# Constant products at the start, keys split out of PSUM, a sink column, and norm work on POOL, in a one-core decoder layer

## The chip, the core and the metric

The kernel runs on one core of a Trainium2 chip. The metric is the device time of one execution in microseconds. Five engines work beside one another, each with its own queue, in order: TensorE (PE in the profile; its weight loads are PEld), VectorE (DVE), ScalarE (ACT), GpSimd (POOL) and SyncE (SP), which here only issues transfers. Everything is f32; the large products use fp32r, a form that TensorE takes in one pass, and each operand is split into a high and a low part so that three products (high x high, high x low, low x high) keep the precision. Plain f32 products take two passes, which the profile counts as two instructions.

## The reference

One decoder layer on a sequence of 2048 positions with 1024 features: a conditioned RMSNorm, one projection into eleven groups of columns, a gated linear attention (4 heads), a sliding-window attention (8 query heads, 2 key heads, window 128) with a sink logit per head, an output projection with a gate, a residual and a last RMSNorm. What the change touches:

```python
mod = silu(c) @ w_ada + b_ada;  shift, scale, gate = split(mod, 3)
h = rmsnorm(x, g_norm) * (1 + scale) + shift
proj = h @ w_in                       # gq gk gv ga gz sq sk sv sz
...
q, k = rope(sq), rope(sk)
scores = where(valid, q @ k.T * hd ** -0.5, -inf)      # blocks of 128 queries, 256 keys
probs = softmax(concat([scores, sink], -1), -1)[..., :-1]
o_swa = (probs @ v) * silu(sz)
...
x = x + gate * (concat([o_gla, o_swa]) @ w_out);  out = rmsnorm(x, g_final)
```

## The kernel before

The sequence is cut into four units of 512 positions (u = 0 to 3), each of four tiles of 128 (t). A unit runs its projections slot by slot, in `ORDER0` for the first unit and `ORDER` for the others; when the slots that an attention needs are there, its tiles follow. In the end `out_tile` runs the output projection for 16 tiles (products py).

**The order of the work.** No engine's order is the order of the program text. Every operation is recorded by the class `Order` with an estimated duration, its dependencies and the queue it belongs to, and `issue()` (lines 209 to 291) then plays the whole program through in a small model: it takes each engine's next ready operation by a key (program position, lowered by `LIFT` for urgent ones) and writes the engines' final orders out of that. In the text below this is the planner. An edit anywhere may so change the order anywhere. The model knows that TensorE, VectorE and so on are free at certain times, that a transfer lands at least 2 us after its issue and that transfers share one wire (`begin`, lines 298 to 327); it takes TensorE to be at full clock from the start. On the chip each engine keeps the planned order and waits where the plan was too early. Since one helper records all operations, nearly all rows of the profile carry the lines L377 (engines and transfers), L424 (products) and L429 (transposes); the tiles' names tell them apart.

**The start** (lines 439 to 575, 718 to 760, 843 to 860, 1246 to 1268). `ones` and `ident` are made on POOL. `silu_rows` spreads silu(c) over all partitions by 16 products (pb). `norm0_start` squares x of the first unit on ScalarE and VectorE and sums the squares over the partitions by four f32 products of 512 columns (ss), then runs `warm(WARM, i)`: 13 constant f32 products of 128 x 128 (pw), whose result nobody reads and which wait for the last ss. ScalarE makes 1/rms of ss by a logarithm and an exponential. `ada_cols` multiplies w_ada (wa) by the silu rows on VectorE, with a sum for each column, and gives the columns `ashift` and `amul`. Then `proj_t_outer` goes through k = 0 to 7, each step with a load of wa (1 MB) and of weights (wr_first), the scaling of x (xt), the split into hh and hl, and 36 products (po) into six PSUM tiles (for k = 0 in two halves).

**The next units' norm** (`norm`, `rsqrt`, lines 708 to 716 and 763 to 795). For units 1 to 3 the sums of squares (sq) are added and scaled (ss), 1/rms comes from a logarithm and an exponential on ScalarE and one Newton step (tiles nwt and rr), all on [128, 4], the small ones on VectorE. Diagonals dgh and dgl and two products (pr) spread the result.

**The keys** (`k_rows`, lines 1061 to 1079). Once per unit four transposes put the rotated keys of both key heads into a PSUM tile (pkr, tag pqk), 64 partitions for each head. ScalarE copies it to kt in SBUF. For each head kst holds a high and a low part, each on all 128 partitions, with the head's 64 rows twice: ScalarE casts the high part to the head's own half, POOL copies it to the other half, and VectorE subtracts twice for the low part, once for each half. The tag pqk has one buffer, which pq of the attention tiles and several others use too.

**The attention tiles** (`swa_tile`, lines 1089 to 1163; 2 heads x 16 tiles). Two transposes bring the queries into PSUM (pq), which become qs. Eight products with kst give the scores (psc); ScalarE copies one half of the band to s, VectorE overwrites the masked places by the other half (`copy_predicated`). VectorE takes the row maximum (mx) and makes nm, the lesser of -mx/8 and the negated sink; the sink's own exponential es is made from sk + nm; ScalarE's four exponentials sum up den, VectorE adds es and inverts, POOL multiplies s by it. Transposes (ppt), a split, triangular masks on POOL and the products with v (ppo) follow.

`load_small` (lines 458 to 465) loads the sinks and negates them (nsk) on VectorE.

Of the kernel before, what the change touches and what calls it, by code (L numbers as in the profile page):

```python
# [8 lines left out]
F32 = mybir.dt.float32  # L9
F32R = mybir.dt.float32r  # L10
I32 = mybir.dt.int32
AF = mybir.ActivationFunctionType
ALU = mybir.AluOpType
AX = mybir.AxisListType
# [3 lines left out]
P = 128  # L18
D = 1024
S = 2048  # L20
KT = D // P
NB = 512
NU = S // NB
TPU = NB // P
EPS = 1e-6
# [30 lines left out]
ORDER = ['sz0', 'kv', 'sq0', 'qk0', 'gv0', 'gz0', 'sq1', 'sz1', 'qk1', 'gv1', 'gz1']  # L56
LATE_AT = 'sz0'
WO_EARLY, WO_LATE = (0, 1, 2, 3), (4, 5, 6, 7)
WARM = 13
WITH_V = (1, 3, 5, 7)  # L60
GT = 4
LIFT = 600
# [320 lines left out]
def layer_kernel(ctx, tc, x, xT, w_ada, w_gate, b_cols, b_gate, g_cols, c_cols, pos, inv_freq,  # L383
                 w_in, w_dec, g_head, sinks, w_out, g_fin, out):
    nc = tc.nc
    od = Order(tc)
    V, A, G, SY = [Engine(od, e) for e in ("V", "A", "G", "SP")]
# [11 lines left out]
    const = Pool("const", 1)  # L399
# [9 lines left out]
    def f(ap):  # L409
        return ap.bitcast(F32)  # L410


    def mmul(o, l, r, start, stop, bank=None):
        n, m, k = free_size(r), free_size(l), l.shape[0]
        mode = cell = None
        if l.dtype == F32:
            dur = 2 * max(0.107, n / 1200)
            if k <= 64:
                mode, cell = "rows", l.start_partition()
            elif m <= 64:  # L420
                mode, cell = "cols", o.start_partition()
        else:
            dur = max(0.112, n * 1.05 / 2400 + 0.006)
        return od.add("PE", lambda: T.matmul(o, l, r, start=start, stop=stop), dur,  # L424
                      [l, r] + ([] if start else [o]), [bank if start and bank is not None else o],
                      mode=mode, cell=cell)
# [5 lines left out]
    def warm(n, after):  # L432

        p = att.tile([P, P], F32, name="pw", tag="pqk")
        for _ in range(n):
            mmul(p, ones, ident, True, True).deps.add(after)


    c_sb = const.tile([P, KT], F32, name="c_sb")
# [18 lines left out]
    def load_small():  # L458
        gh = const.tile([P, 4], F32, name="gh")
        A.dma_start(gh, g_head)  # L460
        sk = const.tile([P, 8], F32, name="sk")
        A.dma_start(sk, sinks.broadcast_to([P, 8]))
        nsk = const.tile([P, 8], F32, name="nsk")
        V.tensor_scalar(nsk, sk, -1.0, None, op0=ALU.mult)
        return gh, sk, nsk


    pf = const.tile([P, 16], F32, name="pos_f")
# [239 lines left out]
    def rsqrt(r, ms):  # L708

        t = tmp.tile(list(r.shape), F32, name="nwt", tag=f"nwt{r.shape[1]}")  # L710
        A.activation(r, ms, AF.Ln)
        A.activation(r, r, AF.Exp, scale=-0.5)
        V.tensor_tensor(t, r, r, ALU.mult)
        V.tensor_tensor(t, t, ms, ALU.mult)
        V.tensor_scalar(t, t, -0.5, 1.5, op0=ALU.mult, op1=ALU.add)
        V.tensor_tensor(r, r, t, ALU.mult)

    def norm0_start():
        ps = att.tile([P, NB], F32, name="ss", tag="px")
# [43 lines left out]
    def norm(u):  # L763

        sq = tmp.tile([P, TPU, 2], F32, name="sq1", tag="sq1", bufs=1)
        for t in range(TPU):
            for i in range(2):
                xn = stp.tile([P, NB], F32, name=f"xn{t}{i}", tag="xs", bufs=2)
                SY.dma_start(xn, x[u * NB + t * P:u * NB + (t + 1) * P, i * NB:(i + 1) * NB])
                A.activation(xn, xn, AF.Square, accum_out=sq[:, t, i:i + 1])  # L770
        ss = tmp.tile([P, TPU], F32, name="ss1", tag="ss1", bufs=1)
        rr = tmp.tile([P, TPU], F32, name="rr1", tag="rr1", bufs=1)
        V.tensor_tensor(ss, sq[:, :, 0], sq[:, :, 1], ALU.add)
        V.tensor_scalar(ss, ss, 1.0 / D, EPS, op0=ALU.mult, op1=ALU.add)
        rsqrt(rr, ss)
        dg = [near.tile([P, TPU, P], F32R, name="dgh", tag="ge", bufs=1),
              stp.tile([P, TPU, P], F32R, name="dgl", tag="xs", bufs=2)]
        for t in range(TPU):
            V.tensor_scalar(dg[0][:, t], ident, rr[:, t:t + 1], None, op0=ALU.mult)
            V.scalar_tensor_tensor(dg[1][:, t], ident, rr[:, t:t + 1], f(dg[0][:, t]),  # L780
                                   op0=ALU.mult, op1=ALU.subtract)
        r = keep.tile([P, NB], F32, name="rstd1", tag="r1")
        pr = att.tile([P, NB], F32, name="pr", tag="px")
        for i in range(2):
            mmul(pr, ones_r, dg[i].rearrange("p a b -> p (a b)"), i == 0, i == 1)
        A.copy(r, pr)
        nh, nl = [], []
        nexth[u] = (nh, nl)
        for j in range(KT):
            nh.append(hp.tile([P, NB], F32R, name=f"hh{u}_{j}", tag="hh"))  # L790
            nl.append(hp.tile([P, NB], F32R, name=f"hl{u}_{j}", tag="hl"))
            xt = stp.tile([P, NB], F32, name=f"xt1_{j}", tag="xs", bufs=2)
            SY.dma_start(xt, xT[:, u, j])
            G.tensor_tensor(xt, xt, r, ALU.mult)
            h_split(j, xt, nh[j], nl[j], V.tensor_copy)
# [235 lines left out]
    vs = {}  # L1031
    szs = {}

    def sink_kv(u):
        def sink(t, ps):
            tt = u * TPU + t
            kt = keep.tile([P, 2, 2, 64], F32, name="kr", tag="kr", bufs=2)
            v = keep.tile([P, 2, 2, 2, 64], F32R, name="vs", tag="v", bufs=VB)
            rope(kt, ps[:, :, 0:128].rearrange("p t (h d) -> p t h d", h=2), 2, tt)
            pv = ps[:, :, 128:256].rearrange("p t (h d) -> p t h d", h=2)  # L1040
            A.copy(v[:, :, :, 0], pv)
            V.tensor_tensor(v[:, :, :, 1], pv, f(v[:, :, :, 0]), ALU.subtract)
            for i in range(2):
                kr[tt + i] = kt[:, i]
                vs[tt + i] = v[:, i]
        return sink

    def sink_sz(kv):
# [12 lines left out]
    def k_rows(u):  # L1061

        if u > 0:
            for kv in range(2):
                for i in range(2):
                    G.tensor_copy(kst[kv][i][:, 0:P], f(kst[kv][i][:, 4 * P:]))
        pt = att.tile([P, NB], F32, name="pkr", tag="pqk")
        for t in range(TPU):
            trans(pt[:, t * P:(t + 1) * P], kr[u * TPU + t].rearrange("p a b -> p (a b)"))
        half = slice(0, 64), slice(64, 128)  # L1070
        kt = near.tile([P, NB], F32, name="kt", tag="ge", bufs=1)
        A.copy(kt, pt)
        for kv in range(2):
            src = half[kv]
            kh, kl = [x[:, P:] for x in kst[kv]]
            A.copy(kh[src], kt[src])
            G.tensor_copy(kh[half[1 - kv]], kt[src])
            for h in half:
                V.tensor_tensor(kl[h], kt[src], f(kh[src]), ALU.subtract)

    def sink_sq(u, kv, qr_of):
        def sink(t, ps):
# [6 lines left out]
    def swa_tile(u, kv, t, qr_of):  # L1089
# [10 lines left out]
        for h, (a, b_) in enumerate(((lo, hi), (hi, lo))):  # L1100
            A.copy(qs[a, h::2], pq[a])
            V.tensor_tensor(qs[b_, h::2], pq[a], f(qs[a, h::2]), ALU.subtract)
        s = tmp.tile([P, 4, P], F32, name="s", tag="s_s", bufs=2)
        j0 = t * P if not first else P
        nj = 2 * P if not first else P
        for pr in range(2):
            ps = att.tile([P, 2, 2 * P], F32, name="psc", tag="psc", bufs=2)
            for h2 in range(2):
                h = 2 * pr + h2
                dst = ps[:, h2, 2 * P - nj:]  # L1110
                mmul(dst, qs[:, h], kh[:, j0:j0 + nj], True, False)
                mmul(dst, qs[:, h], kl[:, j0:j0 + nj], False, True)
            sp = s[:, 2 * pr:2 * pr + 2]
            A.copy(sp, ps[:, :, P:])
            if first:
                G.affine_select(sp, sp, pattern=[[0, 2], [-1, P]], base=0, channel_multiplier=1,
                                compare_op=ALU.is_ge, fill=-3.0e38)
            else:
                V.copy_predicated(sp, m_ex.unsqueeze(1).broadcast_to([P, 2, P]), ps[:, :, :P])
        mx = tmp.tile([P, 4], F32, name="mx", tag="mx")  # L1120
        V.tensor_reduce(mx, s, AX.X, ALU.max)
        hs = slice(4 * kv, 4 * kv + 4)
        nm = tmp.tile([P, 4], F32, name="nm", tag="nm")
        V.scalar_tensor_tensor(nm, mx, -0.125, nsk[:, hs], op0=ALU.mult, op1=ALU.min)
        es = tmp.tile([P, 4], F32, name="es", tag="es")
        V.tensor_tensor(es, sk[:, hs], nm, ALU.add)
        A.activation(es, es, AF.Exp)
        den = tmp.tile([P, 4], F32, name="den", tag="den")
        for h in range(4):
            A.activation(s[:, h], s[:, h], AF.Exp, bias=nm[:, h:h + 1], scale=0.125,  # L1130
                         accum_out=den[:, h:h + 1])
        V.tensor_tensor(den, den, es, ALU.add)
        V.reciprocal(den, den)
        G.tensor_tensor(s, s, den.unsqueeze(2).broadcast_to([P, 4, P]), ALU.mult)

# [94 lines left out]
    def loader(i, lift=LIFT):  # L1230

        if i < len(todo):
# [10 lines left out]
                    w[4](k, k + 4)  # L1243
            od.lift = 0

    srow = silu_rows()
    norm0_start()
    pos_i = rope_load()
    b1 = const.tile([P, KT], F32, name="b1")
    V.tensor_scalar(b1, b_sb[:, :, 1], 1.0, None, op0=ALU.add)  # L1250
    V.tensor_tensor(b1, b1, g_sb, ALU.mult)
    gh, sk, nsk = load_small()
    wk, w_load, w_part, w_keep = first_w()

    def first_k(k):
# [137 lines left out]
```

## Time and profile before

| | |
|---|---|
| runs | 873.1, 873.64, 873.64 us (median 873.64) |
| profiled execution | 872.5 us, of it the span from first to last instruction 870.8 us |
| TensorE products busy | 841.4 us (97%), 5122 instructions |
| TensorE weight loads busy | 732.0 us (84%) |
| VectorE busy | 578.7 us (66%) |
| ScalarE busy | 470.8 us (54%) |
| POOL busy | 374.6 us (43%) |
| moved by transfers | 179.90 MB, 207 GB/s over the span |
| mean granted TensorE clock | 0.994 |

A row of a timeline reads: start, duration in us, engine, line, operation, output<-inputs, shapes, count, and in brackets the idle time of the engine ahead of it with what ended it. Matmuls overlap, so a product's own duration is longer than the distance to the next one; the distance is what counts. A row of the view by stretches reads: stretch, its length, then for PE, PEld, DVE, ACT and POOL the busy time (and instructions), the granted clock, the busy share of the transfer engines and GB/s. Groups by line read: busy time, mean ns, and the idle time ahead of them. Rows of transfers end with the KB of each and the median time from issue to landing.

### The profile page before, as it was taken

The page shows a single profiled execution, that of the slowest core. Times are in us where ns is not written, and L with a number is a line of the kernel's source. Part 1 is how long each engine was busy: PE and PEld are TensorE (multiplying, and loading weights), DVE is VectorE, ACT ScalarE, POOL GpSimd, SP SyncE. Part 2 cuts the span into 40 slices and gives each one's busy share as a digit, 9 for nine tenths or more (in the row PEclk, how much of TensorE's full clock was granted, in tenths as well). Part 3 has the DMA queues.
Part 4 walks back from the last instruction along what each step waited for, and adds up shares of the span by engine and source line. Part 5 has one row for each costly group of instructions (what it writes and reads, how often), then busy time and mean ns, then how long its engine had stood idle before and what let it go on. Part 6 is the DMA issues. An engine that isn't in the chain of part 4 may idle for free. (4 is left out here: it accounts for less than half of the span.)

```text
span 870.8 us, 14663 instructions
## 1 busy us (share of the span) xinstructions
PE 841.4 (97%) x5122; PEld 732.0 (84%) x5122; DVE 578.7 (66%) x1132; ACT 470.8 (54%) x1178; POOL 374.6 (43%) x436
## 2 busy tenths in 40 slices
PE   6999989999999999999999999998999999999997
PEld 4788979789898887898897989887879888888886
DVE  4997699877575577767447786877766654444442
ACT  3677657686464577646536655464386633333332
POOL 2621346658446345744425565244337242222221
PEclk9999999999999999999999999999999999999999
DMA  8969996774443466545337564759474864444421
GB/s 340 324 255 329 352 358 227 275 276 142 152 182 116 154 238 227 204 130 195 124 116 260 191 221 162 256 204 345 147 260 158 302 193 146 145 145 145 146 73 48
DMA packets 76000, 179.90 MB, mean 207 GB/s; under 512 B 8420, under 2 KB 24855, under 8 KB 72727
## 3 DMA queue, kind: packets, MB, share of 16 engines
q1 hardware_dynamic: 74918, 178.93, 58.5%
q8 instruction: 40, 0.66, 0.3%
q14 instruction: 34, 0.27, 0.1%
q10 hardware_dynamic: 1008, 0.05, 0.1%
HBM read 134.78 MB, written 44.17 MB: 206 GB/s over the span
## 5 line engine op out<-in xcount | busy, mean ns | idle before, releaser
L424 PE MATMUL py<-woh,m 128*128 128x512 f32 (+2 forms) x528 | 160.7, 385 | 0.1
L424 PEld LDWEIGHTS py<-woh,m 128*128 128x128 f32 x528 | 98.4, 188 | 20.1 <-DVE r L377 0.5
L424 PE MATMUL py<-wol,m 128*128 128x512 f32 (+2 forms) x264 | 101.4, 384 | 0.0
L377 POOL TENSOR_TENSOR r<-r,gf 128x512 f32<-128x512 f32 x31 | 45.8, 1480 | 114.6 <-ACT xr L377 111.9
L377 ACT ACTIVATE ge<-ge 128x512 f32<-128x512 f32 x96 | 60.6, 631 | 37.4 <-DVE ge L377 36.2
L424 PE MATMUL pn<-wh_gv,hh 128*128 128x272 f32 (+1 forms) x256 | 73.7, 288 | 0.0
L424 PE MATMUL pn<-wl_sq,hh 128*128 128x256 f32 x256 | 73.5, 288 | 0.2 <-DMA wl_sq<-wc 0.2
L424 PE MATMUL pn<-wh_sq,hl 128*128 128x256 f32 x256 | 73.4, 287 | 0.0
L424 PE MATMUL pn<-wh_gv,hl 128*128 128x272 f32 (+1 forms) x256 | 73.3, 287 | 0.0
L424 PE MATMUL pn<-wl_gv,hh 128*128 128x272 f32 (+1 forms) x256 | 73.3, 287 | 0.0
L424 PE MATMUL pn<-wh_sq,hh 128*128 128x256 f32 x256 | 72.7, 286 | 0.0
L377 DVE TENSOR_TENSOR r<-py,xr 128x512 f32<-128x512 f32 (+2 forms) x33 | 22.3, 675 | 62.5 <-PE py L424 62.5
L377 ACT ACTIVATE s<-s,nm 128x128 f32<-128x128 f32 x128 | 50.1, 393 | 20.7 <-DVE nm L377 20.5
L424 PEld LDWEIGHTS py<-wol,m 128*128 128x128 f32 x264 | 49.6, 188 | 9.7
L377 POOL TENSOR_TENSOR s<-s,den 128x512 f32<-128x512 f32 x32 | 35.6, 1111 | 43.7 <-DVE den L377 31.8
L377 POOL TENSOR_TENSOR xt<-xt,rstd 128x512 f32<-128x512 f32 x27 | 38.0, 1411 | 37.2 <-ACT rstd L377 15.6
L424 PEld LDWEIGHTS pn<-wl_sq,hh 128*128 128x128 f32 x256 | 49.4, 193 | 1.5 <-DMA wl_sq<-wc 0.4
L377 POOL TENSOR_TENSOR qr<-qr,rope 128x256 f32<-128x256 f32 x32 | 27.0, 863 | 54.1 <-DVE rope L377 54.1
L424 PEld LDWEIGHTS pn<-wh_sq,hl 128*128 128x128 f32 x256 | 49.3, 193 | 1.0 <-issue 0.3
L424 PEld LDWEIGHTS pn<-wh_sq,hh 128*128 128x128 f32 x256 | 49.2, 193 | 0.8 <-issue 0.2
L424 PEld LDWEIGHTS pn<-wh_gv,hh 128*128 128x128 f32 x256 | 48.4, 189 | 0.6
L424 PEld LDWEIGHTS pn<-wl_gv,hh 128*128 128x128 f32 x256 | 48.4, 189 | 0.5
(262 smaller groups left out, 2515.9 us busy)
## 6 DMA issues: line engine op xcount, KB each, us to landing
xr<-in_x SPq DMA_DIRECT2D x32, 256.0 KB, 2.8
mr<-mixd SPq DMA_DIRECT2D x16, 512.0 KB, 4.0
out<-r SPq DMA_DIRECT2D x32, 256.0 KB, 2.3
wa<-in_w_ada SPq DMA_DIRECT2D x7, 1024.0 KB, 7.7
xn<-in_x SPq DMA_DIRECT2D x24, 256.0 KB, 4.9
xt<-in_xT SPq DMA_DIRECT2D x24, 256.0 KB, 4.5
wl_sz<-wc SPq DMA_DIRECT2D x12, 512.0 KB, 5.8
wh_sz<-wc SPq DMA_DIRECT2D x12, 512.0 KB, 6.2
```

The source lines that it names most:

```text
L377: return order.add(eng, lambda: real(*args, **kw), dur, ins, outs, lock=lock, nbytes=nbytes)
L424: return od.add("PE", lambda: T.matmul(o, l, r, start=start, stop=stop), dur, [l, r] + ([] if start else [o]), [bank if start and bank is ...
```

## The change

Six edits:

1. `warm(WARM0, None)`, 14 products of `ones` and `ident`, is recorded ahead of everything else on TensorE. They depend on the two constants alone.
2. `k_rows` drops the copy kt. ScalarE casts each head's high part straight from PSUM, VectorE subtracts once per head, also from PSUM, and the other halves are filled by four SyncE transfers from SBUF to SBUF (64 partitions x 2 KB, 128 KB each) per unit.
3. The score tile s gets a 129th column per head, which holds 8 times the sink (written by a ScalarE copy). Maximum and exponential run over 129 columns, so that nm comes of mx alone and den contains the sink; es and the sum den + es are dropped. `load_small` scales sk by 8 in place of negating it.
4. The two products of a score (high and low keys) are recorded as a group that stays together on TensorE.
5. `rsqrt`'s four small operations and the two that make ss in `norm` go from VectorE to POOL.
6. In `sink_kv` two assignments of the program text are swapped; no instruction comes of it.

```diff
-WARM = 13
+WARM0, WARM = 14, 13
...
         for _ in range(n):
-            mmul(p, ones, ident, True, True).deps.add(after)
+            i = mmul(p, ones, ident, True, True)
+            if after is not None:
+                i.deps.add(after)
...
-        nsk = const.tile([P, 8], F32, name="nsk")
-        V.tensor_scalar(nsk, sk, -1.0, None, op0=ALU.mult)
-        return gh, sk, nsk
+        V.tensor_scalar(sk, sk, 8.0, None, op0=ALU.mult)
+        return gh, sk
...
         A.activation(r, r, AF.Exp, scale=-0.5)
-        V.tensor_tensor(t, r, r, ALU.mult)
-        V.tensor_tensor(t, t, ms, ALU.mult)
-        V.tensor_scalar(t, t, -0.5, 1.5, op0=ALU.mult, op1=ALU.add)
-        V.tensor_tensor(r, r, t, ALU.mult)
+        G.tensor_tensor(t, r, r, ALU.mult)
+        G.tensor_tensor(t, t, ms, ALU.mult)
+        G.tensor_scalar(t, t, -0.5, 1.5, op0=ALU.mult, op1=ALU.add)
+        G.tensor_tensor(r, r, t, ALU.mult)
...
-        V.tensor_tensor(ss, sq[:, :, 0], sq[:, :, 1], ALU.add)
-        V.tensor_scalar(ss, ss, 1.0 / D, EPS, op0=ALU.mult, op1=ALU.add)
+        G.tensor_tensor(ss, sq[:, :, 0], sq[:, :, 1], ALU.add)
+        G.tensor_scalar(ss, ss, 1.0 / D, EPS, op0=ALU.mult, op1=ALU.add)
...
-        kt = near.tile([P, NB], F32, name="kt", tag="ge", bufs=1)
-        A.copy(kt, pt)
         for kv in range(2):
-            src = half[kv]
             kh, kl = [x[:, P:] for x in kst[kv]]
-            A.copy(kh[src], kt[src])
-            G.tensor_copy(kh[half[1 - kv]], kt[src])
-            for h in half:
-                V.tensor_tensor(kl[h], kt[src], f(kh[src]), ALU.subtract)
+            A.copy(kh[half[kv]], pt[half[kv]])
+        for kv in range(2):
+            kh, kl = [x[:, P:] for x in kst[kv]]
+            V.tensor_tensor(kl[half[kv]], pt[half[kv]], f(kh[half[kv]]), ALU.subtract)
+        for kv in range(2):
+            for x in kst[kv]:
+                SY.dma_start(f(x[half[1 - kv], P:]), f(x[half[kv], P:]))
...
-        s = tmp.tile([P, 4, P], F32, name="s", tag="s_s", bufs=2)
+        s1 = tmp.tile([P, 4, P + 1], F32, name="s", tag="s_s", bufs=2)
+        s = s1[:, :, 0:P]
+        A.copy(s1[:, :, P], sk[:, 4 * kv:4 * kv + 4])
...
-                mmul(dst, qs[:, h], kh[:, j0:j0 + nj], True, False)
-                mmul(dst, qs[:, h], kl[:, j0:j0 + nj], False, True)
+                with od.together():
+                    mmul(dst, qs[:, h], kh[:, j0:j0 + nj], True, False)
+                    mmul(dst, qs[:, h], kl[:, j0:j0 + nj], False, True)
...
-        V.tensor_reduce(mx, s, AX.X, ALU.max)
-        hs = slice(4 * kv, 4 * kv + 4)
+        V.tensor_reduce(mx, s1, AX.X, ALU.max)
         nm = tmp.tile([P, 4], F32, name="nm", tag="nm")
-        V.scalar_tensor_tensor(nm, mx, -0.125, nsk[:, hs], op0=ALU.mult, op1=ALU.min)
-        es = tmp.tile([P, 4], F32, name="es", tag="es")
-        V.tensor_tensor(es, sk[:, hs], nm, ALU.add)
-        A.activation(es, es, AF.Exp)
+        V.tensor_scalar(nm, mx, -0.125, None, op0=ALU.mult)
         den = tmp.tile([P, 4], F32, name="den", tag="den")
         for h in range(4):
-            A.activation(s[:, h], s[:, h], AF.Exp, bias=nm[:, h:h + 1], scale=0.125,
+            A.activation(s1[:, h], s1[:, h], AF.Exp, bias=nm[:, h:h + 1], scale=0.125,
                          accum_out=den[:, h:h + 1])
-        V.tensor_tensor(den, den, es, ALU.add)
         V.reciprocal(den, den)
...
+    warm(WARM0, None)
     srow = silu_rows()
...
-    gh, sk, nsk = load_small()
+    gh, sk = load_small()
```

More of the change, by code (lines that the diff above doesn't have):

```diff
@@ L1043, in sink @@
             for i in range(2):
+                vs[tt + i] = v[:, i]
+            for i in range(2):
                 kr[tt + i] = kt[:, i]
-                vs[tt + i] = v[:, i]
         return sink
```

## The prediction

> **What bounds the kernel now.** I read the page's first two parts, then the rows of TensorE that have idle time in front of them, then stretches of two microseconds around the long ones.
>
> ```profile
> span 870.8 us, 14663 instructions
> PE 841.4 (97%) x5122; PEld 732.0 (84%) x5122; DVE 578.7 (66%) x1132; ACT 470.8 (54%) x1178; POOL 374.6 (43%) x436
> PEclk9999999999999999999999999999999999999999
> ```
>
> TensorE is busy for 841.4 of 870.8 us, and the change takes no product away. It can gain in three ways only: let TensorE start earlier, shorten its gaps, or let it run faster. The first two show in its timeline:
>
> ```profile
> 7.57 2.05 PE L424 MATMUL ss<-sq,ones_r 128*128 128x512 f32 x2 [7.57 <-DVE s_cl L377]
> 8.63 1.09 PE L424 MATMUL pb<-ident_r,s_ch 128*128 128x128 f32 x1
> ...
> 12.73 5.13 PE L424 MATMUL ss<-sq,ones_r 128*128 128x512 f32 x6
> 17.70 3.06 PE L424 MATMUL pw<-ident,ones_r 128*128 128x128 f32 x26
> 21.39 0.35 PE L424 MATMUL po<-hh,wh_first 128*128 128x256 f32 x1 [0.63 <-ACT hh L377]
> ...
> 114.57 0.41 PE L429 MATMUL pq<-ident,qr 128*128 128x128 f32 x2 [0.65 <-ACT kt L377]
> 121.91 0.41 PE L429 MATMUL pq<-ident,qr 128*128 128x128 f32 x2 [2.15 <-DVE qs L377]
> ...
> 607.71 0.88 PE L429 MATMUL pk<-ident,qk 128*128 128x128 f32 x4 [2.80 <-DVE qk L377]
> ```
>
> Real work (po) starts only at 21.39 us. Before it TensorE does the sums of squares (ss), the rows of silu(c) (pb) and 13 constant products (pw, 26 passes, since an f32 product is two). A 512-column pass of ss takes 5.13/6 = 0.855 us, which is 0.214 us per 128 columns; a 128-column pass of pw takes 3.06/26 = 0.118 us. The same array at 0.214 and then at about 0.11: it ran at half clock until about 17.6 us. The page's clock line shows full clock there; I go by the spacing. The gaps cost clock too:
>
> ```profile
> 122.00:124.00 2.00, 2.00 (x9) 1.65 (x10) 1.93 (x4) 1.36 (x3) 0.00 (x0) 0.81 0.59 139
> 124.00:126.00 2.00, 2.00 (x8) 1.71 (x8) 1.98 (x8) 0.00 (x0) 0.00 (x0) 0.50 1.00 383
> 126.00:128.00 2.00, 2.00 (x15) 1.92 (x15) 0.62 (x4) 1.38 (x4) 1.10 (x4) 0.83 0.99 349
> ...
> 608.00:610.00 2.00, 2.00 (x11) 2.00 (x9) 0.17 (x1) 1.63 (x3) 0.00 (x0) 0.50 0.55 213
> ```
>
> The column after the engines is the granted clock. Behind the 2.15 us gap it loses 2 x (0.19 + 0.50 + 0.17) = 1.7 us of full speed; behind the 2.80 us gap it falls to 0.50 as well. A gap above two microseconds therefore costs itself and about 1.7 us more.
>
> **The start.** The 14 new products need `ones` and `ident` alone:
>
> ```profile
> 1.77 0.30 POOL L377 CAST ones_r<-up_ex 128x128 fp32r<-128x128 f32 x1
> ```
>
> They can run from about 2.2 us. They are 28 passes: 28 x 0.214 = 6.0 us if the clock stays at half, so to 8.2 us at worst, 0.6 us past the first ss at 7.57; 28 x 0.118 = 3.3 us at full clock. Before, the clock rose only after a long run of ss passes; the pb products leave the array half empty (a 128-column product each 4.10/16 = 0.26 us between 8.63 and 12.73). The pw passes are as dense as ss, so I let the clock be up by about 8 us. Then ss ends 7.57 + 0.86 = 8.4, the 16 pb take 2.05 and end at 10.5, and the other three ss take 2.56 and end at 13.0 instead of 17.86. What is late next:
>
> ```profile
> 10.32 0.69 DVE L377 TENSOR_TENSOR sq<-sq,sq 128x512 f32<-128x512 f32 x1
> 12.96 1.22 DVE L377 SCALAR_TENSOR_TENSOR wa<-wa,pb 128x1024 f32<-128x1024 f32 x1 [1.95 <-PE pb L424]
> 18.55 0.37 ACT L377 ACTIVATE amul<-ada,b,g_sb 128x1 f32<-128x1 f32 x1
> 18.82 0.59 ACT L377 ACTIVATE ss<-rstd 128x512 f32<-128x512 f32 x1
> 19.44 0.69 DVE L377 TENSOR_TENSOR xt<-xt,ss 128x512 f32<-128x512 f32 x1 [4.03 <-ACT ss L377]
> 20.05 1.21 DVE L377 SCALAR_TENSOR_TENSOR wa<-wa,pb 128x1024 f32<-128x1024 f32 x1
> 23.32 1.29 DVE L377 TENSOR_TENSOR hl<-xt,hh 128x256 fp32r<-128x256 f32 x2
> ...
> 8.14 0.43 SPq L377 DMA_DIRECT2D wa<-in_w_ada  x1
> wa<-in_w_ada SPq DMA_DIRECT2D x1, 1024.0 KB, 8.1
> ```
>
> VectorE's last sum ends at 11.0, so the first two wa passes (1.22 each) run 11.1 to 13.6. ScalarE takes amul to 14.1 and the exponential to 14.8; xt is scaled at 14.9 instead of 19.44, 4.5 us earlier. The next wa pass cannot follow at 15.6, because its transfer, issued at 8.14, lands 8.1 us later, at 16.24: it runs at 16.3 instead of 20.05, 3.75 us earlier. hl stands behind it on VectorE, and TensorE needs hl for the last third of the first k-step. The gain is **3.75 us**. Bounds: +0.6 us where the clock does not rise, -4.5 us where the transfer lands earlier. Later steps find their transfers: no idle row of VectorE or ScalarE between 20 and 50 us names one. The issues of further weights wait for buffers that come free earlier by as much.
>
> [...]
>
> **Keys.** Rows of unit 0, ScalarE, VectorE, then TensorE:
>
> ```profile
> 113.86 0.57 ACT L377 COPY kt<-pkr 128x512 f32<-128x512 f32 x1
> 114.45 1.26 ACT L377 CAST kst<-kt 64x512 fp32r<-64x512 f32 x2
> ...
> 114.66 0.67 DVE L377 TENSOR_TENSOR nwt<-rr 128x4 f32<-128x4 f32 x1
> 115.36 1.21 DVE L377 TENSOR_TENSOR nwt<-nwt,ss 128x4 f32<-128x4 f32 x1
> ...
> 117.10 0.58 DVE L377 TENSOR_SCALAR nwt<-nwt 128x4 f32<-128x4 f32 x1
> 117.59 0.68 DVE L377 TENSOR_TENSOR kst<-kt,kst 64x512 fp32r<-64x512 f32 x1
> 118.19 0.56 DVE L377 TENSOR_TENSOR rr<-rr,nwt 128x4 f32<-128x4 f32 x1
> 118.77 2.11 DVE L377 TENSOR_TENSOR kst<-kt,kst 64x512 fp32r<-64x512 f32 x3
> 120.91 0.86 DVE L377 TENSOR_TENSOR qs<-pq,qs 64x256 fp32r<-64x256 f32 x2
> ...
> 125.06 1.77 PE L424 MATMUL psc<-kst,qs 128*128 128x128 f32 x8
> ```
>
> The qs of 120.91 is what the 2.15 us gap waits for. Ahead of it VectorE loses four norm operations (0.67 + 1.21 + 0.58 + 0.56 = 3.0 us) and two of four kst subtractions (about 1.4 us): qs can come some 4.4 us earlier, more than the gap. The gap goes, and with it the loss of clock: **-3.85 us** (0 if the new order puts pq earlier as well). Against it, the transposed keys in PSUM are read by four operations instead of one copy. The two ScalarE ones end at about 113.86 + 1.26 = 115.1, VectorE's second subtraction at 115.8 or a little more, where the copy ended at 114.43. pq uses the same PSUM buffer and was already late by 0.65 us. Behind it on TensorE stand sz products that could cover the wait if ordered first: 0 to 1.4, I take **+0.7**.
>
> The other half of the keys now comes by four 128 KB transfers per unit, four units. SyncE issues in order, so weight loads behind them wait until VectorE's subtraction is done. The trace has no such transfer; the nearest by size, and the nearest by load (110 to 114 us):
>
> ```profile
> mixd<-o SPq DMA_DIRECT2D x32, 128.0 KB, 3.2
> ...
> wr_sq<-in_w_in SPq DMA_DIRECT2D x2, 256.0 KB, 6.7
> ...
> 236.64 3.42 DVE L377 TENSOR_TENSOR kst<-kt,kst 64x512 fp32r<-64x512 f32 x4 [1.32 <-ACT kst L377]
> ...
> 240.66 1.41 PE L424 MATMUL psc<-kst,qs 128*128 128x256 f32 x8
> ```
>
> In unit 1 two subtractions end at 236.64 + 1.7 = 238.3, the four issues (0.43 each) at about 240, and the copies land between 243 and 247, where psc began at 240.66: 2.5 to 6 us later. The sq projection runs meanwhile, and the planner counts a transfer's time when it orders psc, so cover exists; for what it misjudges I take **+1.0** over all units. Bounds: 0, and 6 + 1.7 in each of two units with no cover.
>
> [...]
>
> **Sink column and norm on POOL.** Per attention tile VectorE loses two sums and reads the sinks nowhere:
>
> ```profile
> L377 DVE TENSOR_TENSOR es<-sk,nm 128x4 f32<-128x4 f32 x32 | 10.3, 322 | 0.6
> ```
>
> ScalarE trades an exponential of four columns for a copy of four. This lies under TensorE: 0. Not covered it would be worth 0.3 us or so per tile where psc waits for VectorE. Rows of 129 columns might slow POOL's normalization; POOL is busy 43% and nothing there sets the pace. POOL's six small operations have no row; between the 0.30 us of the ones_r cast and the 1.21 us that VectorE needed in competition, they take 1.8 to 7 us per unit, and their result was used after 124 us: 0. Copying sk in place of negating it is one operation for one.
>
> **Sum.** The profiled execution took 872.5 us (span 870.8 and 1.7 around it): 872.5 - 3.75 - 3.85 + 0.7 + 1.0 = 866.6. The median of the runs, 873.64, is 1.14 above it, so **867.7 us**.
>
> **Rivals.**
> 1. The start alone. The stall of unit 0 only moves, for the whole order is planned anew: 867.7 + 3.85 = 871.5. For it: it arises because VectorE is later than planned. Against: 4.4 us of its work go.
> 2. Not what it says: the clock stays down. Then +0.6 instead of -3.75: 867.7 + 4.35 = 872.1. For it: TensorE had been busy for ten microseconds before the clock rose. Against: only the half-empty pb lie in between.
> 3. The copies decide, slower. In units 0 and 1 psc stands in TensorE's order ahead of products that could run, and waits 6 us for the landing, with 1.7 us of clock each: 867.7 - 1.0 + 2 x 7.7 = 882.1. It decides once the two waits together exceed what the start and the stall bring, 3.75 + 3.85 - 0.7 = 6.9 us. For it: loads near there took 6.7 us. Against: the whole sq projection stands between keys and scores.
> 4. A new gap above two microseconds somewhere in the new order, with its clock: 867.7 + 2.2 + 1.7 = 871.6.
> 5. The late gap at 607 goes as well, since VectorE has less to do: 867.7 - 2.8 - 1.7 = 863.2.
>
> **Chances.** Forecast 0.50, rivals 0.18, 0.07, 0.09, 0.08 and 0.08. 0.2% is 1.75 us, about what a measurement here can tell from nothing, so faster means below 871.9. Of the forecast nearly all is faster, of rivals 1 and 4 some 0.6, of 2 a third, of 5 all: 0.75. Same takes most of the rest, 0.15; slower is rival 3 and the edge of 2, 0.10. The range goes from rival 5 to a little past rival 2: 863 to 874.
>
> **What would show it.** Right: pw ahead of ss from about 2 us, ss passes 0.43 us apart, po near 17 us; no idle row above one microsecond for pq near 116, granted clock 1.00 there; psc of units 0 and 1 without a transfer as releaser. Wrong: ss at 0.855 as before; psc waiting for kst from SyncE's queue; idle time of POOL's norm in front of the next unit's pr.

## The result, and the profile after

The changed kernel takes 868.48 us (median of 8 runs, 867.38 to 871.49), the kernel before, measured beside it, 874.46 us. The ratio is 0.9932 with a 95% interval of 0.9916 to 0.9948: 4.5 to 7.3 us faster, 5.9 us in the middle. Forecast were 867.7 us and a gain of 5.9 us. The profiled execution took 867.81 us with a span of 866.1 us, 4.7 us under that of before.

The total came out; several of its terms did not. The start of the changed kernel, TensorE's rows of the timeline:

```profile
2.11 5.32 PE L424 MATMUL pw<-ident,ones_r 128*128 128x128 f32 x28 [2.11 <-POOL ones_r L377]
7.44 1.12 PE L424 MATMUL ss<-sq,ones_r 128*128 128x512 f32 x2
...
10.14 2.79 PE L424 MATMUL ss<-sq,ones_r 128*128 128x512 f32 x6
...
16.99 0.36 PE L424 MATMUL po<-hh,wh_first 128*128 128x256 f32 x1 [1.16 <-ACT hh L377]
...
20.57 0.50 PE L424 MATMUL po<-hl,wh_first 128*128 128x256 f32 x2 [0.48 <-DVE hl L377]
...
24.43 0.50 PE L424 MATMUL po<-hh,wh_first 128*128 128x512 f32 x1 [1.47 <-ACT hh L377]
```

The constant products fill 2.1 to 7.4 us. The six late passes of ss now take 2.79 us, 0.46 each, where they took 5.13: the clock is open (by its record from 6.18 us on). Real work starts at 16.99 instead of 21.39. But the products of k = 1 start at 24.43, and before they stood here:

```profile
27.11 0.50 PE L424 MATMUL po<-hh,wh_first 128*128 128x512 f32 x1 [1.18 <-ACT hh L377]
```

So 4.4 us at the first product have become 2.7 us four microseconds of work later. This pair of executions is a favourable one. By the records of the granted clock, it opens at 17.4 us in the one before and between 15.2 and 17.2 us in the five other profiles whose start has no new products of any kind; the products of k = 1 start in these six between 25.98 and 27.11 us. In the six profiles with the new products and the start as in the changed kernel they start between 23.91 and 24.73 us. The means lie 2.2 us apart. VectorE's rows of the changed kernel say where the rest went:

```profile
15.04 0.69 DVE L377 TENSOR_TENSOR xt<-xt,ss 128x512 f32<-128x512 f32 x1 [0.94 <-ACT ss L377]
16.64 1.22 DVE L377 SCALAR_TENSOR_TENSOR wa<-wa,pb 128x1024 f32<-128x1024 f32 x1 [0.91 <-DMA wa<-in_w_ada]
...
19.48 2.45 DVE L377 TENSOR_TENSOR hl<-xt,hh 128x256 fp32r<-128x256 f32 x2
```

The wa pass waits for its transfer, as forecast (16.64 us against 16.3). hl starts 3.84 us earlier than before (23.32), but its two halves take 2.45 us where they took 1.29. POOL is at work beside them in both traces; in the last experiment below, where it is idle meanwhile, they take 0.92 us.

The gaps behind it, TensorE's rows with the longest idle time near 120 and 605, and the same two stretches of 20 us of both kernels (before first; busy PE, PEld, DVE, ACT, POOL, then the granted clock):

```profile
113.13 0.41 PE L429 MATMUL pq<-ident,qr 128*128 128x128 f32 x2 [0.43 <-DVE kst L377]
121.24 0.41 PE L429 MATMUL pq<-ident,qr 128*128 128x128 f32 x2 [1.08 <-DVE qs L377]
...
491.46 0.71 PE L424 MATMUL psc<-kst,qs 128*128 128x256 f32 x4 [1.29 <-DVE s L377]
...
604.72 0.63 PE L429 MATMUL pk<-ident,qk 128*128 128x128 f32 x4 [1.72 <-DVE qk L377]
```

```profile
110.00:130.00 20.00, 17.21 (x86) 14.12 (x86) 18.15 (x37) 11.24 (x26) 8.21 (x12) 0.91 0.95 354
600.00:620.00 20.00, 17.04 (x127) 15.91 (x125) 14.65 (x24) 8.29 (x16) 7.08 (x8) 0.91 0.53 196
```

```profile
110.00:130.00 20.00, 17.88 (x105) 15.07 (x104) 17.75 (x35) 12.76 (x31) 8.37 (x14) 1.00 1.02 357
600.00:620.00 20.00, 18.28 (x149) 16.64 (x148) 16.96 (x28) 9.21 (x16) 4.96 (x5) 1.00 0.64 224
```

The gap of 2.15 us has become 1.08, the one of 2.80 has become 1.72, and behind neither does the clock fall. The clock's records show 3.41 us at half clock in each place before, so 1.7 us less is lost in each. The gap at 491 is new, and there are others below one microsecond. The keys' copies, the view of transfers (KB, median us from issue to landing):

```profile
kst<-kst SPq DMA_DIRECT2D x16, 128.0 KB, 4.0
```

They land after 2.5 to 5.4 us, and no psc waits for one: its idle rows name VectorE only.

### The profile page after: what moved, and what is told of

It is laid out like the page before. It is cut to its first block, busy times and chain, and to the rows that moved or that the text cites. A ratio compares the mean times of both kernels' runs of the same rounds, so it can differ in the third digit from the quotient of the medians.

```text
span 866.1 us, 14643 instructions
## 1 busy us (share of the span) xinstructions
PE 839.6 (97%) x5150; PEld 731.7 (84%) x5150; DVE 555.5 (64%) x1042; ACT 469.1 (54%) x1174; POOL 361.7 (42%) x446
## 4 chain that ended last, share of the span: by engine, by line
PE 61%; DVE 15%; DMA 12%; ACT 7%; issue 3%; POOL 1%; SPq 0%; ACTq 0%; DVEq 0%; POOLq 0%
PE py L424 20%; PE pn L424 17%; PE pt L424 9%; PE po L424 5%; DMA wor<-in_w_out 3%; PE psc L424 3%; PE ppo L424 2%; DVE ge L377 2%; DMA xt<-in_xT 2%; ACT ge L377 2%; DMA wg<-in_w_gate 2%; DVE hl L377 1%; DVE gate L377 1%; ACT s L377 1%; DMA xn<-in_x 1%
## 5 line engine op out<-in xcount | busy, mean ns | idle before, releaser
L377 POOL TENSOR_TENSOR o<-o,zs 128x128 f32<-128x128 f32 x64 | 33.2, 540 | 59.7 <-DVE o L377 59.5
L377 ACT ACTIVATE s<-s,nm 128x129 f32<-128x129 f32 x128 | 51.0, 400 | 12.0 <-DVE nm L377 11.0
L424 PE MATMUL psc<-kst,qs 128*128 128x256 f32 (+1 forms) x256 | 44.1, 291 | 6.3 <-DVE s L377 3.9
L424 PEld LDWEIGHTS psc<-kst,qs 128*128 128x128 f32 x256 | 36.3, 188 | 16.1 <-issue 5.3
```

Source lines behind the costliest of these rows:

```text
L377: return order.add(eng, lambda: real(*args, **kw), dur, ins, outs, lock=lock, nbytes=nbytes)
```

## The experiments

Each run's ratio is to the kernel before on the same chip, with its 95% interval. First each edit alone on the kernel before, then the changed kernel with one part taken back, then the mechanism.

| kernel | ratio to before | interval |
|---|---|---|
| changed kernel | 0.9932 | 0.9916 to 0.9948 |
| products at the start alone | 0.9970 | 0.9954 to 0.9986 |
| keys alone | 0.9965 | 0.9950 to 0.9980 |
| sink column alone | 0.9978 | 0.9964 to 0.9993 |
| norm on POOL alone | 0.9989 | 0.9973 to 1.0004 |
| start and keys | 0.9964 | 0.9939 to 0.9989 |
| changed, no products at the start | 0.9961 | 0.9947 to 0.9975 |
| changed, keys as before | 0.9992 | 0.9977 to 1.0007 |
| changed, sinks as before | 0.9942 | 0.9919 to 0.9965 |
| changed, norm on VectorE | 0.9912 | 0.9879 to 0.9945 |
| half-empty products at the start alone | 0.9986 | 0.9970 to 1.0002 |
| products in the gap near 607 alone | 0.9985 | 0.9961 to 1.0010 |
| changed, order at the start altered | 0.9929 | 0.9909 to 0.9949 |

**The products at the start alone.**

```diff
+    warm(WARM0, None)
     srow = silu_rows()
```

> The kernel before with the 14 constant products at the start and nothing else. Theory (the clock opens early, the transfer of the second wa and VectorE then set the pace): ss passes about 0.43 us apart, first po near 17.0 instead of 21.39, the products of k = 1 near 24.4 instead of 27.11, and from there on the whole program 2.7 us earlier in the same order. The losses of clock near 120 and 605 stay, so 2.7 us of gain (0.3%). Rival A (the start carries the whole change): 6 us of gain. Rival B (the gain is given back, because later work waits for transfers): less than 1 us.

Measured: 872.33 us against 875.1, ratio 0.9970, 2.6 us. That is the theory's size. TensorE's rows of this run:

```profile
16.69 0.36 PE L424 MATMUL po<-hh,wh_first 128*128 128x256 f32 x1 [0.75 <-ACT hh L377]
...
23.91 0.69 PE L424 MATMUL po<-hh,wh_first 128*128 128x512 f32 x1 [1.47 <-ACT hh L377]
...
119.64 0.66 PE L429 MATMUL pq<-ident,qr 128*128 128x128 f32 x2 [3.03 <-DVE qs L377]
...
607.27 0.66 PE L429 MATMUL pk<-ident,qk 128*128 128x128 f32 x4 [2.84 <-DVE qk L377]
```

The start moves as in the whole change, and both long gaps stay. In this execution the clock also fell right at 24 us, behind two waits of 0.45 and 1.47 us (last section); its span of 871.0 us is no shorter than before. The gain is therefore not the same in each execution. Rival A (the start carries all) is out, and rival B needs a gain under 1 us, which the interval (1.2 to 4.0 us) excludes.

**The keys alone** (with the score's two products kept together, edit 4, as in the run with the sink column; no run has edit 4 by itself).

```diff
-        A.copy(kt, pt)
...
+            A.copy(kh[half[kv]], pt[half[kv]])
...
+            for x in kst[kv]:
+                SY.dma_start(f(x[half[1 - kv], P:]), f(x[half[kv], P:]))
```

> The kernel before with the keys split from PSUM and copied by transfers, and the two products of a score kept together. Theory: VectorE's subtractions ahead of the first qs halve (about 1.4 us), the gap near 121.9 shrinks below two microseconds and its loss of clock (1.7 us) goes, while the copies make some scores wait: between 3 us faster and no change. Rival (the copies decide): psc waits for transfers in units 0 and 1, 2 us or more slower.

Measured: 872.74 against 875.1, ratio 0.9965, 3.1 us faster. TensorE's rows:

```profile
115.00 0.41 PE L429 MATMUL pq<-ident,qr 128*128 128x128 f32 x2 [0.88 <-DVE kst L377]
...
606.93 0.63 PE L429 MATMUL pk<-ident,qk 128*128 128x128 f32 x4 [1.68 <-DVE qk L377]
```

The gap near 121.9 is gone, the one near 607 has shrunk to 1.68, and the mean granted clock of the span is 0.998 instead of 0.994. In this execution the one edit removes both losses of clock. Over its twelve executions the mean clock is 0.9958, against 0.9938 for the kernel before on that chip; the difference is worth about 1.7 of the 3.1 us, as an estimate (0.0020 x 870 us). The rival (psc waits for the copies) shows nowhere.

**The sink column alone.**

```diff
-        V.tensor_tensor(es, sk[:, hs], nm, ALU.add)
-        A.activation(es, es, AF.Exp)
...
-        V.tensor_tensor(den, den, es, ALU.add)
```

> The kernel before with the sink as a 129th column and the two products of a score kept together. Theory: VectorE loses about 21 us of small operations over 32 tiles, TensorE hardly waits for them: no change, within 1.5 us. Rival (VectorE's small operations are what the late gaps wait for): the gap of 2.80 us near 607 falls below two microseconds and loses no clock, 2 to 3 us faster.

Measured: 873.82 against 875.1, ratio 0.9978, 1.9 us, interval 0.6 to 3.2. That lies between theory and rival. The late gap is gone, but the one near 120 is longer and a new one stands near 176:

```profile
121.86 0.41 PE L429 MATMUL pq<-ident,qr 128*128 128x128 f32 x2 [2.84 <-DVE qs L377]
...
176.18 0.74 PE L424 MATMUL psc<-kst,qs 128*128 128x256 f32 x4 [2.34 <-ACT s L377]
...
605.84 0.50 PE L424 MATMUL pg<-ga,ones_r 128*128 128x512 f32 x1 [1.11 <-ACT ga L377]
```

So the clock falls in two windows here too (at 123.0 and 177.6 us), and this trace does not show where the gain comes from. Over the twelve executions the mean clock is 0.9950 against 0.9938, about 1.0 us by the same estimate.

**The norm on POOL alone.**

```diff
-        V.tensor_tensor(t, r, r, ALU.mult)
+        G.tensor_tensor(t, r, r, ALU.mult)
```

> The kernel before with the norm's small operations on POOL. Theory: the four operations ahead of the qs of 120.91 leave VectorE (3.0 us), so the gap of 2.15 us near 121.9 goes and with it the loss of clock: 2 to 4 us faster. [...]

Measured: 874.66 against 875.1, ratio 0.9989; no change is inside the interval. The gap the norm was to close:

```profile
121.04 0.41 PE L429 MATMUL pq<-ident,qr 128*128 128x128 f32 x2 [1.95 <-DVE qs L377]
```

It is 1.95 us instead of 2.15, though 3.0 us of small operations left VectorE. Taking them away hardly brought qs forward. VectorE's rows ahead of that qs:

```profile
115.13 1.54 DVE L377 TENSOR_TENSOR wl_sq<-wr_sq,wh_sq 128x512 fp32r<-128x512 f32 x1 [1.00 <-ACT kst L377]
116.59 3.41 DVE L377 TENSOR_TENSOR kst<-kt,kst 64x512 fp32r<-64x512 f32 x4
```

VectorE now waits 1.00 us for ScalarE's kst, wl_sq takes 1.54 us where it took 0.68, and the four subtractions take 3.41 us where they took 2.79. So some 2.5 of the 3.0 us came back as waiting and as longer operations.

**The changed kernel without the products at the start.**

```diff
-    warm(WARM0, None)
```

> The changed kernel without the 14 products at the start. Theory (the start is worth 2.7 us by itself, and less of it survives beside the other edits, because the single edits add up to 8.6 us against the 6.0 us of the whole change): 2 to 3 us slower than the changed kernel, so 3 to 4 us faster than before; po at about 20 us, gaps behind it as in the changed kernel. Rival (the start carries the change, the rest gives nothing): no faster than before.

Measured: 871.2 us against 874.46, ratio 0.9961. The start is worth 0.0029 (2.5 us) in the changed kernel, about as much as alone. The first real work:

```profile
20.49 0.36 PE L424 MATMUL po<-hh,wh_first 128*128 128x256 f32 x1 [0.63 <-ACT hh L377]
```

**The changed kernel with the keys as before.**

```diff
-            A.copy(kh[half[kv]], pt[half[kv]])
+        A.copy(kt, pt)
```

> The changed kernel with k_rows as it was. Theory (the keys take VectorE's subtractions away ahead of the first attention tile, which is one of two edits that do so): the gap near 120 stays short or loses its clock, 0 to 3 us slower than the changed kernel. Rival (the transfers cost what the subtractions save): no slower, or faster by 1 us.

Measured: 873.99 against 874.46, ratio 0.9992. Without the keys the whole change is gone: they are worth 0.0060, 5.2 us. Theory's bound of 3 us was too low, and the rival (the transfers eat the saving) is out. TensorE's rows of that run, and the clock behind the second of them:

```profile
117.64 0.41 PE L429 MATMUL pq<-ident,qr 128*128 128x128 f32 x2 [1.73 <-DVE qs L377]
...
152.98 0.77 PE L424 MATMUL psc<-kst,qs 128*128 128x256 f32 x4 [2.15 <-DVE s L377]
...
189.49 0.39 PE L424 MATMUL pn<-wh_kv,hh 128*128 128x256 f32 x1 [2.00 <-ACT zs L377]
...
612.83 0.66 PE L429 MATMUL pk<-ident,qk 128*128 128x128 f32 x4 [3.20 <-DVE qk L377]
...
154.00:156.00 2.00, 2.00 (x10) 1.90 (x10) 1.43 (x2) 0.51 (x4) 1.84 (x2) 0.50 0.95 399
```

The last three rows of TensorE are gaps of two microseconds and more, each with a fall of the clock; behind the first row, 1.73 us, it held. Over the twelve executions the mean clock, 0.9942, is that of the kernel before.

**The changed kernel with the sinks as before.**

```diff
-        V.tensor_scalar(nm, mx, -0.125, None, op0=ALU.mult)
+        V.scalar_tensor_tensor(nm, mx, -0.125, nsk[:, hs], op0=ALU.mult, op1=ALU.min)
```

> The changed kernel with the sinks' exponential and sums as before. Theory (the sink column matters by VectorE's share ahead of the gaps, and the gaps near 120 and 605 are already below two microseconds): 0 to 2 us slower than the changed kernel; if the gap near 605 grows over two microseconds, 1.7 to 3 us slower. Rival (it is off TensorE's path): no change.

Measured: 868.26 against 873.68, ratio 0.9942, within the interval of the changed kernel's 0.9932. The late gap is longer again, but in this execution the clock held behind it:

```profile
604.75 0.63 PE L429 MATMUL pk<-ident,qk 128*128 128x128 f32 x4 [2.35 <-DVE qk L377]
```

Over the twelve executions the mean clock is 0.9954, between the 0.9946 of the kernel before on that chip and the 0.9968 of the changed kernel, so it does not always hold. What the sink column gives alone, the keys give for the most part already.

**The changed kernel with the norm on VectorE.**

```diff
-        G.tensor_tensor(ss, sq[:, :, 0], sq[:, :, 1], ALU.add)
+        V.tensor_tensor(ss, sq[:, :, 0], sq[:, :, 1], ALU.add)
```

> The changed kernel with the norm's small operations on VectorE. Theory (they stand ahead of the qs that the gap near 120 waits for, 3.0 us of VectorE): that gap grows above two microseconds and loses clock, 2 to 3 us slower than the changed kernel. Rival (halving the subtractions is enough): no change.

Measured: 865.58 us against 873.68, ratio 0.9912. It is not slower; it is the fastest of all kernels run, though its interval overlaps the changed kernel's. Near 120 the longest idle row is

```profile
114.56 0.41 PE L429 MATMUL pq<-ident,qr 128*128 128x128 f32 x2 [0.94 <-DVE kst L377]
```

so the keys' edit is enough, and the norm's move is not needed for it. The four norm operations, 3.0 us beside POOL's copies of the keys in the kernel before, take 0.95 us on VectorE here (0.47 + 0.15 + 0.17 + 0.16), where those copies are gone.

**Start and keys together, without sink column and norm.**

```diff
+    warm(WARM0, None)
...
+            A.copy(kh[half[kv]], pt[half[kv]])
```

> The kernel before with the products at the start and the keys from PSUM (scores kept together), without the sink column and the norm on POOL. Theory (start and keys carry the change, 2.6 and 3.1 us by themselves): 5 to 6 us faster than before, like the whole change. Rival (the small operations of VectorE are needed as well): 3 to 4 us faster, with a gap above two microseconds near 120 or 605.

Measured: 869.97 against 873.68, ratio 0.9964. The interval reaches from 1.0 to 5.3 us and decides between neither. Its profile (span 863.9 us, late gap 1.41 us, clock 0.997), which is that of the fastest of its twelve executions, speaks for the theory, its median for the rival. The question stays open.

**Half-empty products at the start.** 28 products of one pass in fp32r stand where the 28 f32 passes stood.

```diff
+        for _ in range(2 * n):
+            mmul(p, ones_r, ident_r, True, True)
```

> The kernel before with 28 constant products at the start that take as long but leave the array half empty: one pass each in fp32r (ident_r by ones_r), like pb. Theory (the clock follows the density of the products): it opens no earlier than before, ss passes stay 0.855 us apart or become fast only late, po near 21 us, no gain. Rival (any busy window opens the clock): ss passes 0.43 us apart from about 9 us, po near 17 us, 2.7 us faster, like the run with the start alone.

Measured: 872.96 against 874.46, ratio 0.9986. TensorE's rows:

```profile
2.11 6.24 PE L424 MATMUL pv<-ident_r,ones_r 128*128 128x128 f32 x28 [2.11 <-POOL ones_r L377]
8.15 2.02 PE L424 MATMUL ss<-sq,ones_r 128*128 128x512 f32 x2
...
13.27 3.96 PE L424 MATMUL ss<-sq,ones_r 128*128 128x512 f32 x6
...
20.76 0.36 PE L424 MATMUL po<-hh,wh_first 128*128 128x256 f32 x1 [0.63 <-ACT hh L377]
```

TensorE is busy from 2.1 us on without a pause, and still the first ss runs at half clock (2.02 us for its two passes, 1.12 in the changed kernel) and po begins near 21 us. The clock opened at 15.60 us, partway through the late ss. The rival (any busy window opens it) is out: the time for which products ran did not decide here. That the array is half empty can be read from the distances, as an estimate. At half clock, from 25.66 us on in the kernel with the norm on VectorE, fp32r products of 512 columns stand 0.43 us apart, 0.107 per 128 columns; these of 128 columns stand 0.22 apart (6.24 / 28), so for half of the time no column enters. The form, fp32r against f32, did not decide either: in that same run nothing but such dense fp32r products runs from 25.23 us on, and from 29.06 us on, where three take 0.69 us, they stand 0.23 us apart again. So in these runs the clock opened with the density of the products.

**Products in the late gap.** Eight constant products ahead of the pk of unit 3; all other instructions keep their order.

```diff
+            if (u, pair) == (NU - 1, 0):
+                for _ in range(8):
+                    mmul(pk[:, 0:P], ones, ident, True, True).dur = 0.0
             for i in range(4):
                 trans(pk[:, i * P:(i + 1) * P], k3[:, i])
```

> The kernel before with 8 constant products of 128 x 128 ahead of the four transposes pk of unit 3, in the place of the 2.80 us gap near 607; every other instruction keeps its place in its engine's order. Theory (a gap costs its length and 1.7 us of clock behind it): the gap stays, the products fill 1.7 us of it, the granted clock stays at 1.00 there, and the run is up to 1.7 us (0.2%) faster although it does more work. Rival (the clock behind the gap costs nothing, since other engines set the pace there): no change, or slower by the products' time.

Measured: 872.29 against 873.68, ratio 0.9985; the interval holds no change. The place itself is clearer. Two products on either side of the gap, before and in this run:

```profile
587.61 0.28 PE L429 MATMUL gaT<-ident,ga 128*32 128x128 f32 x1 [1.31 <-ACT ga L377]
...
637.71 0.44 PE L429 MATMUL pq<-ident,qr 128*128 128x128 f32 x2 [0.21 <-ACT ort L377]
```

```profile
588.90 0.29 PE L429 MATMUL gaT<-ident,ga 128*32 128x128 f32 x1 [1.31 <-ACT ga L377]
...
606.22 1.95 PE L424 MATMUL pk<-ident,ones_r 128*128 128x128 f32 x16
608.67 0.66 PE L429 MATMUL pk<-ident,qk 128*128 128x128 f32 x4 [0.51 <-DVE qk L377]
...
637.61 0.44 PE L429 MATMUL pq<-ident,qr 128*128 128x128 f32 x2 [0.64 <-ACT ort L377]
...
608.00:610.00 2.00, 1.49 (x13) 1.33 (x12) 1.22 (x3) 0.68 (x2) 0.00 (x0) 1.00 0.99 362
```

Between the two products lie 50.10 us before and 48.71 us here, 1.4 us less, with 16 more passes; the granted clock stays at 1.00 where it was 0.50. Of the 1.4 us, 1.1 were won behind the pk (30.00 us from there to the pq before, 28.94 here), although the pq waits 0.43 us longer. On this execution's grid (last section) 606.22 to 608.67 us lies in one window, which without the products would have been idle for 2.45 us. Over the twelve executions the mean clock is 0.9958 against 0.9946, about 1.0 us by the estimate above. In this place the work after the gap paid for the gap's idleness, and the products spared it 1.1 us of that without shortening the gap.

**The order at the start altered.** The sinks' scaling goes from VectorE to POOL behind the start, and POOL scales xt for k = 2, 4, 6 only after the hl before it.

```diff
+    G.tensor_scalar(sk, sk, 8.0, None, op0=ALU.mult).deps.add(ready[0])
...
+            i.deps.add(ready[0])
```

> The changed kernel with two orders altered at the start: the scaling of the sinks leaves VectorE for POOL, behind the start, and POOL's scaling of xt for k = 2, 4, 6 waits for the hl before it. Theory (after the clock, VectorE's hl of k = 0 is what TensorE waits for, 2.45 us instead of 0.83 while POOL works beside it): hl ends about 2 us earlier, the waits for hl (0.48 and 0.45 us) and part of the 1.47 us ahead of k = 1 go, 1 to 2.5 us faster than the changed kernel. Rival (the second wa's transfer sets the pace): no change.

Measured: 868.55 against 874.46, ratio 0.9929: as the changed kernel. The waits for hl are gone and k = 1 starts at 21.96 instead of 24.43, 2.5 us earlier; but two other waits have come in the same unit (VectorE's hl first, then TensorE's rows):

```profile
17.76 0.92 DVE L377 TENSOR_TENSOR hl<-xt,hh 128x256 fp32r<-128x256 f32 x2
...
21.96 0.50 PE L424 MATMUL po<-hh,wh_first 128*128 128x512 f32 x1 [0.52 <-ACT hh L377]
...
62.73 0.39 PE L424 MATMUL pn<-wh_gv,hh 128*128 128x272 f32 x1 [1.12 <-ACT ga L377]
72.98 0.47 PE L424 MATMUL pz<-gat,wd 96*128 96x512 f32 x1 [1.09 <-DVE gat L377]
```

So the theory held at its place: the slow hl cost TensorE what it said, and the transfer did not set the pace. The time did not change all the same. The two waits, 2.2 us, are for ScalarE and VectorE; the pz of the second starts at 73.23 in the changed kernel, so that 0.25 us of the lead is left there. In this execution the clock also falls at 148.7 us, behind waits of 1.09 and 0.66 us, which it does not in the changed kernel's. That the two waits came because TensorE ran ahead of these engines is likely, not shown, since the order was planned anew there too.

## Why the prediction was right

**The mechanism of the start** was right: the clock opened on the dense products (at 6.18 us), ss end at 12.8 us (forecast 13.0), xt is scaled at 15.04 (14.9), po starts at 16.99, and in the run with half-empty products, which run no shorter, it opened only at 15.60. **Its size** was too large: 3.75 us were forecast; it is 2.7 us in the two traces, 2.2 between the means of six profiles each, 2.6 and 2.5 in the two comparisons of time. The term that failed is "hl stands behind it on VectorE ... 3.75 us earlier": hl did start 3.84 us earlier, but at 2.45 us it ended only 2.7 us earlier. I had priced the moved operation by its duration in the old neighbourhood. The spacing of pb was misread too: from the second on they stand 0.21 us apart, not 0.26.

**The stall of unit 0** was put at -3.85 us. The gap and its clock went down by 1.07 + 1.7 = 2.8 us. What I named as its main cause, the norm's four operations, is wrong: the norm alone leaves 1.95 us of gap, since 2.5 of the 3.0 us come back as waiting for ScalarE and as longer operations, and the kernel with the norm back on VectorE has no such gap. The keys' edit, of which I counted only two subtractions at 1.4 of the 4.4 us, is what it hung on; with the keys as before the whole change gains nothing. That edit also takes POOL's two copies away, 2.12 us at 116.62 in the trace of before, beside the norm operations and the subtractions. Which of the two parts does it, no run separates.

**Costs of the keys**, +0.7 for pq and +1.0 for the copies: neither came. pq's wait went from 0.65 to 0.43 us. It did start later behind the keys' transposes, 4.06 us instead of 2.64, but TensorE's new order has 13 sz products in between where there were 6, the cover that the prediction named. And no score waited for a copy, although these took 4.0 us (forecast 3.2 to 6.7). Rival 3 had its transfer times right and its waiting wrong.

**The sinks at nothing** was wrong when taken alone (1.9 us, interval 0.6 to 3.2) and not distinguishable from right inside the change (0.9942 against 0.9932).

**Rival 5**, the late gap, had a chance of 0.08 and came in part: 2.80 to 1.72 us, and 1.7 us of clock. It makes up for the smaller start. Sum by the two traces: 2.7 (start) + 2 x 1.7 (clock) + 1.1 + 1.1 (the two gaps) + 0.2 (pq) = 8.5 us, of a span shorter by 4.7. About 3.8 us went back. TensorE's idle rows behind the first 31 us sum to 12.5 us before (18 rows) and to 13.3 after (24 rows), although the two gaps and pq gave up 2.4: some 3.2 us are new, shorter gaps, such as 1.29 us at 491. The last 0.6 us I cannot place. These are two executions out of many: over all executions whose clock is on record its mean is 0.9968 with the change and 0.9938 to 0.9946 without, which puts the clock's part nearer to 2.3 us than to 3.4, as an estimate (0.0026 x 870). The single edits show the same from the other side: 0.30 + 0.35 + 0.22 + 0.11 = 0.98%, of which the whole change keeps 0.68%. Keys and sink column each shorten the same late gap, which can be won once.

So the right total is in part luck. The start and the stall each brought about 1 us less than forecast, the costs of 1.7 us did not come, the late gap brought 2.8 us that were not counted, and the new gaps took 3.2 us that were not counted either; these errors happen to cancel.

## What to carry to other kernels

When TensorE is 97% busy, ask of each gap not only how long it is but whether it, with the waits beside it, is long enough to cost clock behind it: shortening 2.2 us to 1.1 was worth 2.8 us in the trace. Price a moved operation by its new neighbours, and take an edit's credit from a run with that edit alone or taken back, since edits that shorten the same queue do not add. The constant products that opened the clock early here were dense (6.18 us); behind half-empty ones that ran no shorter it opened at 15.60. Where constant products stood in a gap, they cost nothing that the runs could tell (0.9985, interval 0.9961 to 1.0010).

## What the runs showed of the hardware

In these profiles the falls of the clock went with the idle time in a stretch (window) of 3.41 us, not with the length of one gap. In the trace of before the record of the granted clock opens at 17.43 us, falls at 123.25 and 607.94 and is back at 126.66 and 611.35: 3.41 us at half each time, and from change to change 31, 1, 141 and 1 times 3.413 us. With the keys as before the distances of the products show three falls, at 153.5, 191.0 and 614.3 us, 11 and 124 such steps apart. The place of this grid against the program differs from execution to execution. I laid the idle rows (start less idle time) on it for the 14 kernels that were profiled. Once the clock was open, every window with 1.75 us of idle time or more was followed by one at half clock (2.07 and 2.80 us before; 3.01, 2.84 and 1.92 with the start alone; 2.15, 1.89 and 1.97 with the keys as before), every one with 1.66 or less by full clock. At 1.70 us (norm on VectorE, at 25 us) it fell, at 1.71 us (keys as before, norm on POOL alone) it did not. A limit of two microseconds for one gap, as the prediction had it, does not fit these rows: a gap of 2.35 us kept its clock (sinks as before), where the grid cut it into 1.50 and the rest, and the clock fell at 24 us with the start alone, where waits of 0.45 and 1.47 us add up to 1.92 in one window. The start opened the clock at 15.2 to 17.4 us without the new products, with the place of the grid; that this is a reason why the time of one kernel differs from run to run is likely, not shown.

The opening went with fuller windows. The 28 dense passes opened the clock at 6.18 us in the changed kernel and between 5.3 and 8.1 us in all seven profiles that have them; 28 half-empty ones, without a pause from 2.11 to 8.15 us, did not. The latest is the kernel with the norm on VectorE: a window from 1.23 to 4.64 us held 2.52 us of dense passes, three quarters of it, and left the clock at half, and the full window behind it opened it. With the half-empty products, a window of 1.1 us of pb and 2.3 us of ss (12.19 to 15.60 us) opened it.
